# Strassen's output projection in layer B: raw weights and attention outputs loaded ahead of their splits

## The chip, the cores and the metric

The kernel runs on one core of a Trainium2 chip. The metric is the device time of one execution in microseconds. An A/B difference under about 0.2% (4 us here) can't be told from none.

## The reference

One inference step of two encoder layers over 2048 prompt tokens and 64 sample tokens, width 1024. Each layer is

```python
h = rms_norm(x, norm_g)
q, k, v, gate = split(h @ w_in)            # q and k normalised per head
o = attend(q, k, v, bias, band of chunks)  # 16 heads of 64
x = x + (o * silu(gate)) @ w_out           # w_out: 1024 x 1024
```

Layer A attends over its own and 2 earlier chunks of 64 tokens, layer B over its own and 8 earlier. The case concerns the last line for layer B, the output projection `y = x1 + og @ w_out_b` over 2112 tokens, everything in float32 outside the kernel.

## The kernel before, in words

**Precision by splitting.** TensorE multiplies float16. Each float32 operand is split into a high and a low float16 part, and a product is three matmuls: high by high, high by low, low by high. A split is one instruction on ScalarE (`hi = scale * raw`, L2130 for weights, L2192 for attention outputs) and then one on VectorE (`lo = scale * raw - hi`, L2131 and L2195).

**The projection** (`fast_output_jobs`). The tokens are cut into 8 spans of 264 (`OT`). The first two spans are done one by one (`alone`; here "the first block" and "the second block"): for each of 8 output chunks of 128, two products of 12 matmuls of 264 columns, one for each half of the inner dimension. The other six spans are done in three pairs (`group`) by a Strassen scheme with seven products of 12 matmuls for each of 4 output chunks, instead of eight. A *combine* (L2284, VectorE) adds a finished product from PSUM, with a scale, to the residual tile `res` or `more`; after its last combine a tile is stored. Two accumulator banks alternate, so a product can begin only when the combine two before it is done. The first and second block have 8 combines each, every pair 28.

**Operands.** 16 weight tiles of 128 x 512 are split as they are (`plain`), and 16 more are sums and differences of raw weight tiles (`mixed`: four for each output chunk `m`, made on GpSimd, L2153). A pair's outputs need seven tiles of two halves each: four raw quarters per half come into the four `xraw` buffers (`fetch_half`), three subtractions on GpSimd (L2243) change them in place between the splits, and a fourth follows for the last tile. A second half is loaded into the same four buffers.

**What sets the order.** The PE queue is written in program order. All other engines' queues, SP's included (it issues every DMA), are ordered at build time by a scheduler that simulates the program, within its dependences and extra ordering edges (`behind`). Layer B's attention (`pipeline`) interleaves scores, exponentials and P times V with the projections (`filler`). Into each of its steps `drip` puts one or two *steps* of the two chains `drips["x"]` (output splits) and `drips["w"]` (weight splits), x first; a product forces those of its own operands that have not run (`force`). The chain of weights is opened by `held["prepare"]`, called from `scale_work` in the last head pair (hp 7) at its eighth event, once the weight scale is known. Each split step loads its own raw tile (`raw_w`) and splits it:

```python
def plain(m, b):
    def fn():
        st.w[m, b].w = split_w(raw_w(m, b))     # wraw: 3 buffers
    st.w[m, b] = Step("w", fn)
```

Names in the trace: `wraw`, `xraw` raw tiles; `wx`, `ws` (4 buffers each), `wh`, `wl` (12 each) split weights; `xx` (7 buffers), `ph`, `pl`, `values`, `pt` split outputs, the last four tags borrowed from attention; `pj` accumulators; `p` attention scores (3 buffers); `sb` score banks.

Of the kernel before, what the change touches and what calls it, by code (L numbers as in the profile page):

```python
# [14 lines left out]
ALU = mybir.AluOpType  # L15
AX = mybir.AxisListType

P = 128
# [16 lines left out]
WB = 3  # L35
# [4 lines left out]
WN = 12  # L40
# [18 lines left out]
def hybrid_encoder_kernel(  # L59
# [246 lines left out]
    def scale_work(hp, u, e):  # L306
# [20 lines left out]
        elif at == 2:  # L327
            output_top()
        elif at == 3:
            held["chain"].append(output_across)  # L330
        elif at == 5:
            held["chain"].append(output_scales)
        elif at == 8:
            while held["chain"]:
                held["chain"].pop(0)()
            held["prepare"]()
# [1757 lines left out]

    def drip(n=1):
        for _ in range(n):
            for chain in drips.values():
                if chain:
                    chain[0].run()
                    break  # L2100
# [16 lines left out]
    def fast_output_jobs(xin, xout):  # L2117
# [4 lines left out]
        wtags = ["wx"] * 4 + ["wh"] * 4 + ["wl"] * 4 + ["ws"] * 4 + ["wh"] * 8 + ["wl"] * 8  # L2122
        both = 2 * OT
        step = 3 * OT / 2400
        spans = [(0, 1), (1, 1)] + [(2 + 2 * p, 2) for p in range(3)]

# [7 lines left out]
        def raw_w(m, b):  # L2134
            raw = t("wraw", [P, 512], WB)
            load(raw.rearrange("p (k c) -> p k c", k=4), w_o_b[m, :, b])
            return raw

        def plain(m, b):
            def fn():  # L2140
                st.w[m, b].w = split_w(raw_w(m, b))
            st.w[m, b] = Step("w", fn)

        def mixed(m):
            raws = {}

            def put(i, fn):
                def run():
                    st.s[m, i].w = split_w(fn())
                st.s[m, i] = Step("w", run)  # L2150

            def pool(dst, x, y_, op):
                nc.gpsimd.tensor_tensor(raws[dst], raws[x], raws[y_], op=op)  # L2153
                return raws[dst]

            def s1():
                for b in (2, 3, 0):
                    raws[b] = raw_w(m, b)
                return pool(3, 2, 3, ALU.add)

            def s4():
                raws[1] = raw_w(m, 1)
                return pool(1, 1, 0, ALU.subtract)

            put(4, s1)
            put(6, lambda: pool(2, 0, 2, ALU.subtract))
            put(5, lambda: pool(0, 3, 0, ALU.subtract))
            put(2, s4)

        def prepare():  # L2170
            run_all("scales")
            for b in range(0, 4, 2):
                for m in range(4):
                    for e in range(2):
                        plain(m, b + e)
            for m in range(4):
                mixed(m)
# [3 lines left out]
        def fetch(j, n, c):  # L2181
            out = []
            for s in range(n):
# [3 lines left out]
                out.append(raw)  # L2187
            return out
# [20 lines left out]
        def operand(i):  # L2209
# [18 lines left out]
            tags = ["values"] * 3 + ["pt"] * 2 + ["xx"] * 2 if i == 3 else ["xx"] * 5 + ["ph", "pl"]  # L2228
# [6 lines left out]
            def split(y_, k, at, less=()):  # L2235
                def part(e):
                    if k == 0 and e:
                        fetch_half(e)
# [3 lines left out]
                    for o, a, b in less:  # L2242
                        nc.gpsimd.tensor_tensor(raws[e, o], raws[e, a], raws[e, b], op=ALU.subtract)  # L2243
                    split_x(x.parts[y_][:, 2 * e : 2 * e + 2], raws[e, at], tag in ("ph", "pl") and e == 0)
                return part
# [73 lines left out]
        def group(i, x, m):  # L2319
# [6 lines left out]
            for y_, (acc, wi, xi, start, rv) in enumerate((  # L2326
# [7 lines left out]
                if not filler.attending and (y_ % 2 or m == 3):  # L2334
                    drip()
                if wi == 2:
                    store(xout[:, m, rows], top)
                    next_res(i, m)
# [7 lines left out]
        def add_span(i):  # L2346
# [7 lines left out]
            def gen():  # L2354
# [6 lines left out]
                for m in range(4) if n == 2 else range(0, 8, 2):  # L2361
                    if ready(i + 1) and (i or m == 4):
                        st.x[i + 1] = operand(i + 1)
                    yield from (group if n == 2 else alone)(i, x, m)
# [129 lines left out]
```

## Time and profile before

| | us |
|---|---|
| median of 3 runs | 2090.42 (2086.74 to 2090.99) |
| profiled execution | 2088.68 |
| its span, first to last instruction | 2086.9 |
| mean granted TensorE clock | 0.992 |
| first product of the projection starts | 1879.87 |
| last matmul ends about | 2083.3 |
| a matmul of 264 columns, start to start | 0.113 |

In a timeline row stand the start, the duration, the engine, the line, the operation and the tiles written and read; in square brackets the idle time of that engine before it and what ended it. `PE` is TensorE, `DVE` VectorE, `ACT` ScalarE, `POOL` GpSimd, `SPq` the queue that issues DMAs. A row of waits reads: who waited, for whom, total us, times, longest.

### The profile page before, as it was taken

To read this page: it belongs to the slowest core of one execution; us is meant where nothing else is said; L and a number is where in the kernel's file an instruction comes from. 1 tells how busy PE (TensorE), PEld (TensorE's weight loads), DVE (VectorE), ACT (ScalarE), POOL (GpSimd) and SP (SyncE) were. 2 spreads that over 40 slices of the span, in tenths; PEclk is the share of its full clock that TensorE was granted. 3 is DMA by queue.
4 is the path that set the end of the run, shared out by engine and by line. 5 is a ranking of instruction groups with operands and counts; after the bars stand their busy time and mean duration, and the time that the engine had idled before them with its cause. 6 is when DMAs were issued, how large, how long until landed. Compare 5 with 4: busy or idle time off the path is not lost.

```text
span 2086.9 us, 40567 instructions
## 1 busy us (share of the span) xinstructions
PE 1987.4 (95%) x12670; PEld 1416.2 (68%) x12670; DVE 1448.5 (69%) x4111; ACT 1440.5 (69%) x3574; POOL 1191.9 (57%) x1569
## 2 busy tenths in 40 slices
PE   7899999999999999989999999999999999989699
PEld 6787787777888999645555555555555555557578
DVE  7667767767667554778667676776767767687763
ACT  6887888778788332468777787777867778786420
POOL 5665565444457445677566565765756666566620
PEclk9999999999999999999999999999999999999899
DMA  7888877889766776798989798897978878598543
GB/s 258 254 216 229 222 202 207 225 208 271 194 170 169 220 224 196 266 239 219 240 173 242 169 218 200 187 237 168 226 186 199 215 163 184 139 198 189 169 146 105
DMA packets 598168, 424.64 MB, mean 203 GB/s; under 512 B 403952, under 2 KB 527232, under 8 KB 597920
## 3 DMA queue, kind: packets, MB, share of 16 engines
q1 hardware_dynamic: 597952, 422.06, 78.9%
q8 instruction: 100, 1.64, 0.3%
q14 instruction: 116, 0.95, 0.2%
HBM read 253.14 MB, written 73.43 MB: 156 GB/s over the span
## 4 chain that ended last, share of the span: by engine, by line
PE 50%; DVE 10%; DMA 8%; ACT 6%; issue 5%; POOL 2%; SPq 1%; ACTq 0%; POOLq 0%; DVEq 0%
PE pj L758 9%; PE pj L760 9%; PE pj L759 9%; PE o L1847 4%; PE sb L1683 2%; PE sb L1684 2%; PE pj L2059 2%; PE pj L2061 2%; PE pj L2060 2%; PE tp L1011 1%; PE pj L2291 1%; PE pj L2294 1%; PE pj L2295 1%; DVE p L1687 1%; DMA q<-q 1%
## 5 line engine op out<-in xcount | busy, mean ns | idle before, releaser
L758 PE MATMUL pj<-wh,xx 128*128 128x512 f16 (+2 forms) x1648 | 642.2, 390 | 19.7 <-ACT pa L781 4.4
L760 PE MATMUL pj<-wh,xx 128*128 128x512 f16 (+2 forms) x1648 | 624.5, 379 | 0.6 <-POOL xx L640 0.6
L1740 POOL TENSOR_TENSOR values<-p,values 128x640 f16<-128x640 f32 (+4 forms) x256 | 327.0, 1278 | 199.1 <-ACT values L1739 190.6
L759 PE MATMUL pj<-wh,xx 128*128 128x512 f16 x1024 | 388.9, 380 | 1.3 <-DVE wh L545 1.3
L1699 ACT ACTIVATE p<-p,nm 128x640 f32<-128x640 f32 (+5 forms) x264 | 199.5, 756 | 182.4 <-DVE nm L1692 146.6
L1687 DVE CUSTOM_DVE_ANT_0 p<-sb,BT 128x640 f32<-128x640 f32 (+5 forms) x272 | 196.4, 722 | 141.9 <-PE sb L1684 120.5
L640 POOL TENSOR_TENSOR xx<-xraw,xx 128x528 fp32r<-128x528 f32 (+4 forms) x144 | 188.5, 1329 | 94.7 <-ACT xx L639 87.5
L759 PE MATMUL pj<-wl,xx 128*128 128x512 f32 (+1 forms) x624 | 235.3, 377 | 1.5 <-DVE wl L545 1.5
L849 POOL TENSOR_TENSOR f<-f,mhalf 128x4 f32<-128x4 f32 x182 | 186.3, 1024 | 12.2
L760 PEld LDWEIGHTS <-xx 128*128 128x128 f16 x1024 | 100.4, 98 | 124.1 <-issue 2.7
L1347 ACT ACTIVATE p<-p,nm 128x257 f32<-128x257 f32 (+2 forms) x272 | 134.5, 496 | 68.7 <-DVE nm L1336 35.7
L1500 POOL TENSOR_TENSOR o<-gt,o 128x256 f32<-128x256 f32 (+1 forms) x132 | 106.1, 804 | 125.0 <-ACT p L1347 72.7
L1739 ACT CAST values<-p 128x640 f16<-128x640 f32 (+4 forms) x256 | 168.2, 657 | 12.9 <-DMA pt<-values 6.8
L758 PEld LDWEIGHTS <-xx 128*128 128x128 f16 x1024 | 100.3, 98 | 83.8 <-ACT sq L827 1.4
L759 PEld LDWEIGHTS <-xx 128*128 128x128 f16 x1024 | 100.4, 98 | 83.3 <-issue 3.5
L2059 PE MATMUL pj<-xx,wh 128*128 128x264 f32 x512 | 148.5, 290 | 4.3 <-DVE res L2069 1.8
L1847 PEld LDWEIGHTS <-values 128*128 128x128 f16 x1344 | 123.8, 98 | 39.6 <-DMA pt<-values 1.7
L1847 PE MATMUL o<-pt,values 128*128 128x256 f16 (+1 forms) x1344 | 144.7, 256 | 2.2 <-DMA pt<-values 2.2
L2060 PE MATMUL pj<-xx,wh 128*128 128x264 f32 x512 | 145.7, 285 | 0.0
L2061 PE MATMUL pj<-xx,wl 128*128 128x264 f32 x512 | 145.0, 283 | 0.2 <-DVE wl L538 0.2
L758 PEld LDWEIGHTS pj<-wh,xx 128*128 128x128 f32 x624 | 119.2, 191 | 36.9 <-ACT pa L781 8.2
L760 PEld LDWEIGHTS pj<-wh,xx 128*128 128x128 f32 x624 | 119.0, 191 | 23.1
(356 smaller groups left out, 5082.5 us busy)
## 6 DMA issues: line engine op xcount, KB each, us to landing
xx<-xsb SPq DMA_DIRECT2D x112, 512.0 KB, 4.3
xx<-xsa SPq DMA_DIRECT2D x88, 512.0 KB, 4.9
xraw<-oga SPq DMA_DIRECT2D x64, 264.0 KB, 3.8
xsa<-xx SPq DMA_DIRECT2D x32, 512.0 KB, 4.0
wl<-in_w_in_b_dram SPq DMA_DIRECT2D x64, 256.0 KB, 5.1
wraw<-in_w_in_b_dram SPq DMA_DIRECT2D x56, 256.0 KB, 3.6
wraw<-in_w_o_b_dram SPq DMA_DIRECT2D x48, 256.0 KB, 4.0
xraw<-in_x_dram SPq DMA_DIRECT2D x40, 256.0 KB, 4.3
```

The costliest lines, as they stand in the source:

```text
L640: nc.gpsimd.tensor_tensor(lo, rv, wide(hi), op=ALU.subtract)
L758: nc.tensor.matmul(ps[:n, :C], xh, wh, start=k == 0, stop=False)
L759: nc.tensor.matmul(ps[:n, :C], xh, wl, start=False, stop=False)
L760: nc.tensor.matmul(ps[:n, :C], xl, wh, start=False, stop=k == KC - 1)
L849: nc.gpsimd.tensor_tensor(fv, fv, mhalf[:n, :H], op=ALU.pow)
L1687: mi = nc.vector.tensor_tensor_reduce(out=p[r, :nk], in0=S[r, o : o + nk], in1=b, op0=ALU.add, op1=ALU.min, scale=1.0, scalar=3e38, accum_ ...
L1699: ex = nc.scalar.activation(p[:n, :nk], p[:n, :nk], AF.Exp, scale=-1.0, bias=it.nm[:n, c : c + 1], accum_out=it.sm[:n, c : c + 1],)
L1740: lo = nc.gpsimd.tensor_tensor(two[:, :, 1, :], pv, two[:, :, 0, :], op=ALU.subtract)
L1847: nc.tensor.matmul(it.O[:, h * T + q0 : h * T + q1_], held["VH"][:, kt, h], x, start=kt == kb and not low, stop=kt == tb and low == 1,)
L2059: nc.tensor.matmul(ps[:, :OT], wh, oh, start=k == 0, stop=False)
L2060: nc.tensor.matmul(ps[:, :OT], wh, ol, start=False, stop=False)
L2061: nc.tensor.matmul(ps[:, :OT], wl, oh, start=False, stop=k == KC - 1)
```

## The change

- `prepare` runs at the sixth event of the last head pair instead of the eighth, and loads three raw weight tiles itself; every single split then loads the tile three splits ahead (`ahead`).
- The raw tiles of the mixed weights come four at a time, several steps ahead (`late`: after splits 10, 16, 20 and 26), into buffers of their own: `wl` for m 0 and 1, `wraw` and `scan` for 2, `p` and `wraw` for 3.
- `gate_at` keeps a chain from dripping for some ticks after its loads; while x waits, w drips. `pin` adds an ordering edge to the loads and subtractions: not ahead of the latest anchor.
- The tiles' tags come in another order (`ws` second; `ph`, `pl` fourth and fifth).
- In the first block, before its last group (m 6), the second block's remaining splits are forced and the first pair's operand (`operand(2)`) is begun. The second half's raws are asked for at the end of the first half.
- Outside attention a pair drips one step at every product (was: at products 1, 3, 5, and at all in the last group). The next group's residuals are loaded after the third product instead of the sixth.

No arithmetic changes, and the PE queue keeps its order of matmuls in the projection.

```diff
-        elif at == 8:
+        elif at == 6:
             while held["chain"]:
                 held["chain"].pop(0)()
             held["prepare"]()
...
+    gate_at, ticks = {"x": 0, "w": 0}, [0]
+
     def drip(n=1):
+        ticks[0] += 1
         for _ in range(n):
-            for chain in drips.values():
-                if chain:
+            for kind, chain in drips.items():
+                if chain and ticks[0] >= gate_at[kind]:
                     chain[0].run()
                     break
...
-        wtags = ["wx"] * 4 + ["wh"] * 4 + ["wl"] * 4 + ["ws"] * 4 + ["wh"] * 8 + ["wl"] * 8
+        wtags = ["wx"] * 4 + ["ws"] * 4 + ["wh"] * 4 + ["wl"] * 4 + ["wh"] * 8 + ["wl"] * 8
...
+        def pin(x):
+            behind(x.ins, list(bg.anchors.values())[-1])
...
+        def raw_w(key, tag, bufs):
+            cols = 640 if tag == "p" else 512
+            raw = t(tag, [P, cols], bufs)[:, :512]
+            pin(load(raw.rearrange("p (k c) -> p k c", k=4), w_o_b[key[1], :, key[2]]))
+            raws_w[key] = raw
+
+        singles = [(0, m, b + e) for b in range(0, 4, 2) for m in range(4) for e in range(2)]
+
+        def mixed_raws(m):
+            tags = [("wl", WN)] * 4 if m < 2 else [("wraw", WB)] * 3 + [("scan", 1)]
+            if m == 3:
+                tags = [("p", 3)] * 3 + [("wraw", WB)]
+            for b, tag in zip((2, 3, 0, 1), tags):
+                raw_w((1, m, b), *tag)
+
+        ahead = {n: (lambda n=n: raw_w(singles[n + 3], "wraw", WB)) for n in range(13)}
+        late = {10: 0, 16: 1, 20: 2, 26: 3}
+
+        def order_w(store_in, key, fn):
+            n = len(drips["w"])
+
+            def run():
+                store_in[key].w = split_w(fn())
+                if n in ahead:
+                    ahead[n]()
+                if n in late:
+                    mixed_raws(late[n])
+
+            store_in[key] = Step("w", run)
 
         def prepare():
             run_all("scales")
+            for n in range(3):
+                raw_w(singles[n], "wraw", WB)
+            gate_at["w"] = ticks[0] + 2
...
                 held["last"] = load(raw, og[1][:, c : c + 2, o : o + OT]).ins
                 out.append(raw)
+            gate_at["x"] = ticks[0] + (1 if filler.attending else 3)
             return out
...
-            tags = ["values"] * 3 + ["pt"] * 2 + ["xx"] * 2 if i == 3 else ["xx"] * 5 + ["ph", "pl"]
+            tags = ["values"] * 3 + ["pt"] * 2 + ["xx"] * 2 if i == 3 else ["xx"] * 3 + ["ph", "pl"] + ["xx"] * 2
...
-                    if k == 0 and e:
-                        fetch_half(e)
...
+                    if y_ == 5 and e == 0:
+                        fetch_half(1)
...
-                if not filler.attending and (y_ % 2 or m == 3):
+                if not filler.attending:
                     drip()
+                if wi == 5:
+                    next_res(i, m)
                 if wi == 2:
                     store(xout[:, m, rows], top)
-                    next_res(i, m)
...
+                    if i == 0 and m == 6:
+                        for chain in st.x[1].steps.values():
+                            force(*chain)
+                        st.x[2] = operand(2)
```

How the queues come out is shown at two places. The lines of the changed kernel are some higher: L2136 and L2137 are its weight splits, L2204 and L2207 its output splits, L2145 and L2197 the loads of weight and output raws, L2182 and L2253 the subtractions, L2296 the combine, L2279 the residual loads of the single blocks.

The first place is the end of the first block. `res_25682` (after: `res_25712`) takes the eighth combine, the first block's last, and `more_25799` (`more_25837`) the ninth; `p`, `nm` and `o` rows are attention. VectorE before:

```order
L2131 SCALAR_TENSOR_TENSOR wh_25839<-wraw_25548,scl,wh_25839 128x512
L1692 TENSOR_SCALAR nm_25747<-nm_25747 128x1
L2284 SCALAR_TENSOR_TENSOR res_25682<-pj_25844,scl,res_25682 128x264
L2131 SCALAR_TENSOR_TENSOR wh_25880<-wraw_25877,scl,wh_25880 128x512
L1687 ISA p_25930,nm_25747<-sb_25929,BT 128x640
L1687 ISA nm_25747 128x1
L1499 TENSOR_TENSOR o_4936_25900<-o_25786,o_4936_25900 64x256 x2
L1692 TENSOR_SCALAR nm_25747<-nm_25747 128x1
L1811 TENSOR_TENSOR o_4948_25966<-tp_25959,o_4948_25966 64x64 x2
L2284 SCALAR_TENSOR_TENSOR more_25799<-pj_25919,scl,more_25799 128x264
```

VectorE after:

```order
L2207 SCALAR_TENSOR_TENSOR xx_25876<-xraw_25829,scl,xx_25876 128x2x264
L1692 TENSOR_SCALAR nm_25777<-nm_25777 128x1
L2207 SCALAR_TENSOR_TENSOR xx_25879<-xraw_25833,scl,xx_25879 128x2x264
L2296 SCALAR_TENSOR_TENSOR res_25712<-pj_25884,scl,res_25712 128x264
L2207 SCALAR_TENSOR_TENSOR xx_25917<-xraw_25835,scl,xx_25917 128x2x264
L1687 ISA p_25965,nm_25777<-sb_25964,BT 128x640
L1687 ISA nm_25777 128x1
L1499 TENSOR_TENSOR o_4953_25943<-o_25816,o_4953_25943 64x256 x2
L1692 TENSOR_SCALAR nm_25777<-nm_25777 128x1
L1811 TENSOR_TENSOR o_4961_26001<-tp_25994,o_4961_26001 64x64 x2
L2296 SCALAR_TENSOR_TENSOR more_25837<-pj_25954,scl,more_25837 128x264
```

Three splits of the first pair's outputs stand where two splits of mixed weights stood; those weights are split earlier. GpSimd at the same place, from the cast of the last but one score tile on, before:

```order
L1740 TENSOR_TENSOR values_11787<-p_25855,values_11787 128x5x128
L2153 TENSOR_TENSOR wraw_26270<-wraw_26268,wraw_26270 128x512
L1500 TENSOR_TENSOR o_4936_25900<-gt_25898,o_4936_25900 128x256
L2153 TENSOR_TENSOR wraw_26268<-wraw_26272,wraw_26268 128x512
L1812 TENSOR_TENSOR o_4948_25966<-G_25652,o_4948_25966 128x64
L1724 TENSOR_TENSOR G_26018<-pb_25192,sm_25746 128x128 x2
L1740 TENSOR_TENSOR values_11787<-p_25930,values_11787 128x5x128
L2153 TENSOR_TENSOR wraw_26272<-wraw_26270,wraw_26272 128x512
L2243 TENSOR_TENSOR xraw_25909<-xraw_25911,xraw_25909 128x528
```

GpSimd after:

```order
L2253 TENSOR_TENSOR xraw_25829<-xraw_25831,xraw_25829 128x528
L1740 TENSOR_TENSOR values_11787<-p_25895,values_11787 128x5x128
L2253 TENSOR_TENSOR xraw_25831<-xraw_25835,xraw_25831 128x528
L2253 TENSOR_TENSOR xraw_25835<-xraw_25835,xraw_25829 128x528
L1500 TENSOR_TENSOR o_4953_25943<-gt_25941,o_4953_25943 128x256
L1812 TENSOR_TENSOR o_4961_26001<-G_25682,o_4961_26001 128x64
L2182 TENSOR_TENSOR wl_25382<-wl_25386,wl_25382 128x512
L2182 TENSOR_TENSOR wraw_25623<-wraw_25621,wraw_25623 128x512
L1724 TENSOR_TENSOR G_26053<-pb_25217,sm_25776 128x128 x2
L2253 TENSOR_TENSOR xraw_25833<-xraw_25833,xraw_25835 128x528
L1740 TENSOR_TENSOR values_11787<-p_25965,values_11787 128x5x128
```

The first pair's subtractions stand up to eight rows further forward, one ahead of the cast. ScalarE there, after (before, no split stood between the two exponentials but that of `wh_25839`):

```order
L2204 ACTIVATE xx_25876<-xraw_25829,scl 128x2x264
L2204 ACTIVATE xx_25879<-xraw_25833,scl 128x2x264
L1699 ACTIVATE p_25895,sm_25776<-p_25895,nm_25777 128x640
L1495 COPY o_4953_25943<-o_25816 64x256 x2
L1739 CAST values_11787<-p_25895 128x5x128
L2204 ACTIVATE xx_25917<-xraw_25835,scl 128x2x264
```

Two output splits moved ahead of the last exponential but one. SP's queue where the first pair's raws are issued, before:

```order
L2316 DMA out_dram<-res_25436 128x2x264
L2186 DMA xraw_25909<-ogb 128x2x264
L1507 DMA ogb<-o_4895_25616 128x256
L2186 DMA xraw_25911<-ogb 128x2x264
L2267 DMA res_25917<-x_99 128x2x264
L2316 DMA out_dram<-more_25560 128x2x264
L2267 DMA more_26008<-x_99 128x2x264
L2186 DMA xraw_25913<-ogb 128x2x264
L2186 DMA xraw_25915<-ogb 128x2x264
```

SP after:

```order
L2328 DMA out_dram<-res_25465 128x2x264
L1748 DMA_TRANSPOSE pt_25649<-values_11787 128x10x128
L2197 DMA xraw_25829<-ogb 128x2x264
L2197 DMA xraw_25831<-ogb 128x2x264
L2279 DMA res_25952<-x_99 128x2x264
L2328 DMA out_dram<-more_25582 128x2x264
L2279 DMA more_26043<-x_99 128x2x264
L2197 DMA xraw_25833<-ogb 128x2x264
L2197 DMA xraw_25835<-ogb 128x2x264
```

The four raws keep their place among the stores and reloads. The second place is in the second block, VectorE from its third combine (`res`, the eleventh of all) on. Before:

```order
L2284 SCALAR_TENSOR_TENSOR res_25917<-pj_26010,scl,res_25917 128x264
L2131 SCALAR_TENSOR_TENSOR wh_26430<-wraw_26272,scl,wh_26430 128x512
L2195 SCALAR_TENSOR_TENSOR ph_26060<-xraw_25911,scl,ph_26060 128x2x264
L2284 SCALAR_TENSOR_TENSOR res_25917<-pj_26050,scl,res_25917 128x264
L2195 SCALAR_TENSOR_TENSOR xx_26024<-xraw_25915,scl,xx_26024 128x2x264
```

After:

```order
L2296 SCALAR_TENSOR_TENSOR res_25952<-pj_26045,scl,res_25952 128x264
L2207 SCALAR_TENSOR_TENSOR xx_25876<-xraw_26060,scl,xx_25876 128x2x264
L2207 SCALAR_TENSOR_TENSOR xx_26056<-xraw_25833,scl,xx_26056 128x2x264
L2207 SCALAR_TENSOR_TENSOR xx_25879<-xraw_26064,scl,xx_25879 128x2x264
L2296 SCALAR_TENSOR_TENSOR res_25952<-pj_26092,scl,res_25952 128x264
```

The second half's splits have come forward to between these two combines; `xraw_26064` takes over a buffer of the first half.

More of the change, by code (lines that the diff above doesn't have):

```diff
@@ L2132, in split_w @@
             return w
[L2134 to L2168, printed above, removed]
+        raws_w = {}
@@ L2170, in prepare @@
+        ahead = {n: (lambda n=n: raw_w(singles[n + 3], "wraw", WB)) for n in range(13)}
[9 more added lines that the diff above has]
+            store_in[key] = Step("w", run)
         def prepare():
             run_all("scales")
[L2172 to L2175, printed above, removed]
@@ L2176, in prepare, with pool @@
-            for m in range(4):
-                mixed(m)
+            for n in range(3):
+                raw_w(singles[n], "wraw", WB)
+            gate_at["w"] = ticks[0] + 2
+            for key in singles:
+                order_w(st.w, key[1:], lambda key=key: raws_w[key])
+            for m in range(4):
+                def pool(dst, x, y_, op, m=m):
+                    r = [raws_w.get((1, m, b)) for b in (dst, x, y_)]
+                    pin(nc.gpsimd.tensor_tensor(*r, op=op))
+                    return r[0]
+                order_w(st.s, (m, 4), lambda pool=pool: pool(3, 2, 3, ALU.add))
+                order_w(st.s, (m, 6), lambda pool=pool: pool(2, 0, 2, ALU.subtract))
+                order_w(st.s, (m, 5), lambda pool=pool: pool(0, 3, 0, ALU.subtract))
+                order_w(st.s, (m, 2), lambda pool=pool: pool(1, 1, 0, ALU.subtract))
@@ L2242, in part @@
                     for o, a, b in less:
-                        nc.gpsimd.tensor_tensor(raws[e, o], raws[e, a], raws[e, b], op=ALU.subtract)
+                        pin(nc.gpsimd.tensor_tensor(raws[e, o], raws[e, a], raws[e, b], op=ALU.subtract))
                     split_x(x.parts[y_][:, 2 * e : 2 * e + 2], raws[e, at], tag in ("ph", "pl") and e == 0)
+                    if y_ == 5 and e == 0:
+                        fetch_half(1)
                 return part
```

## The prediction

> **What bounds the kernel now.** I read the page first: the busy table, then the 40 slices.
>
> ```profile
> PE 1987.4 (95%) x12670; PEld 1416.2 (68%) x12670; DVE 1448.5 (69%) x4111; ACT 1440.5 (69%) x3574; POOL 1191.9 (57%) x1569
> PE   7899999999999999989999999999999999989699
> PEclk9999999999999999999999999999999999999899
> ```
>
> TensorE is busy 95% of the span; apart from the first slice its weakest slice is the third from the end, where layer B's output projection takes over from attention. Everything the change touches lies between 1800 us and the end, so the second view is the same span in stretches (engine busy us, matmul count in brackets, granted clock, DMA share).
>
> ```profile
> 1810.00:1820.00 10.00, 10.00 (x61) 5.71 (x59) 6.82 (x20) 7.76 (x18) 6.13 (x9) 1.00 0.43 91
> 1860.00:1870.00 10.00, 9.96 (x59) 5.46 (x58) 8.68 (x22) 8.51 (x18) 9.67 (x12) 1.00 1.05 187
> 1870.00:1880.00 10.00, 7.93 (x42) 4.20 (x40) 9.33 (x24) 9.78 (x22) 5.51 (x7) 0.85 1.02 248
> 1913.00:1920.00 7.00, 7.00 (x64) 6.07 (x62) 4.56 (x11) 4.95 (x13) 1.71 (x2) 1.00 1.04 221
> 1920.00:1985.00 65.00, 47.08 (x350) 36.58 (x348) 50.64 (x62) 28.49 (x44) 45.49 (x34) 0.89 0.60 162
> 1985.00:1994.00 9.00, 9.00 (x82) 7.83 (x81) 4.72 (x9) 0.73 (x1) 0.52 (x1) 1.00 0.77 240
> 1994.00:2018.00 24.00, 20.04 (x170) 16.33 (x169) 20.08 (x28) 10.07 (x14) 11.48 (x8) 1.00 0.44 136
> 2018.00:2087.00 69.00, 65.27 (x581) 56.53 (x578) 24.43 (x50) 0.00 (x0) 0.00 (x0) 1.00 0.33 107
> ```
>
> (Columns: PE, PEld, DVE, ACT, POOL, clock, DMA, GB/s.) The stretch 1920 to 1985, second block and first pair, loses 65 - 47.08 = 17.9 us of TensorE time, and its clock of 0.89 another 0.11 x 65 = 7.2 us at most. 1994 to 2018 loses 4.0. The rest is full. Who is waited for in the 65 us:
>
> ```profile
> PE pj L2291 <- DVE res L2284: 12.6, 8, 3.4
> POOL wraw L2153 <- DMA wraw<-in_w_o_b_dram: 11.5, 6, 3.8
> ACT values L2192 <- DMA xraw<-ogb: 9.5, 4, 2.9
> DVE wl L2131 <- ACT wl L2130: 4.9, 2, 2.8
> DVE wh L2131 <- ACT wh L2130: 3.5, 2, 3.2
> ```
>
> TensorE waits for combines (L2284: accumulator into the residual). A combine is short; it is late because splits stand ahead of it in VectorE's queue. The groups of that window by line (count | busy us, mean ns | idle before them and its releaser), and then the same few microseconds in GpSimd's and in VectorE's timeline (start, duration):
>
> ```profile
> L2195 DVE SCALAR_TENSOR_TENSOR xx<-xraw,scl,xx 128x528 f16<-128x528 f32 x13 | 15.5, 1217 | 1.3 <-ACT xx L2192 1.2
> L2131 DVE SCALAR_TENSOR_TENSOR wl<-wraw,scl,wl 128x512 f16<-128x512 f32 x8 | 9.1, 1141 | 4.9 <-ACT wl L2130 4.9
> L2195 DVE SCALAR_TENSOR_TENSOR values<-xraw,scl,values 128x528 f16<-128x528 f32 x6 | 5.6, 934 | 3.3 <-ACT values L2192 3.3
> L2131 DVE SCALAR_TENSOR_TENSOR wh<-wraw,scl,wh 128x512 f16<-128x512 f32 x4 | 4.1, 1050 | 3.5 <-ACT wh L2130 3.5
> L2284 DVE SCALAR_TENSOR_TENSOR res<-pj,scl,res 128x264 f32<-128x264 f32 x13 | 6.2, 479 | 0.0
> ...
> L2243 POOL TENSOR_TENSOR xraw<-xraw,xraw 128x528 f32<-128x528 f32 x16 | 23.8, 1485 | 8.4 <-DVE wl L2131 4.1 <-DVE values L2195 2.7 <-DMA xraw<-ogb 1.3
> L2153 POOL TENSOR_TENSOR wraw<-wraw,wraw 128x512 f32<-128x512 f32 x12 | 17.1, 1427 | 14.8 <-DMA wraw<-in_w_o_b_dram 11.5 <-DVE o L1499 3.3
> ```
>
> ```profile
> 1944.57 1.73 POOL L2153 TENSOR_TENSOR wraw<-wraw,wraw 128x512 f32<-128x512 f32 x1
> 1946.26 1.79 POOL L2243 TENSOR_TENSOR xraw<-xraw,xraw 128x528 f32<-128x528 f32 x1
> 1948.02 1.73 POOL L2153 TENSOR_TENSOR wraw<-wraw,wraw 128x512 f32<-128x512 f32 x1
> 1954.94 1.26 POOL L2153 TENSOR_TENSOR wraw<-wraw,wraw 128x512 f32<-128x512 f32 x1 [3.48 <-DMA wraw<-in_w_o_b_dram]
> ```
>
> ```profile
> 1944.34 4.28 DVE L2195 SCALAR_TENSOR_TENSOR xx<-xraw,scl,xx 128x528 f16<-128x528 f32 x3
> 1948.54 1.75 DVE L2131 SCALAR_TENSOR_TENSOR wl<-wraw,scl,wl 128x512 f16<-128x512 f32 x1
> 1976.39 0.73 DVE L2131 SCALAR_TENSOR_TENSOR wl<-wraw,scl,wl 128x512 f16<-128x512 f32 x1
> ```
>
> The weight split takes 0.73 us at 1976, while GpSimd is idle, and 1.75 at 1948, beside a GpSimd subtraction; that subtraction takes 1.26 alone (1954.94) and 1.73 beside the split. The pair side by side costs 1.75 where one after the other would cost 1.99: the two engines nearly take turns. So the stretch is bound by the splits and subtractions together, 42.8 us of splits (the four groups above and 8.5 us in three smaller ones, 38 splits) and 40.9 us of 28 subtractions in 65 us, and to a lesser part by raw tiles that come late.
>
> **The change, part by part.**
>
> Start earlier (event 6 for 8, raws 3 splits ahead). The first weight split moves about four score steps forward, to near 1810, where VectorE has 3.2 us of 10 idle, ScalarE 2.2 and DMA stands at 0.43: cost 0, covered by that slack. Without it each split would cost up to 1.75. Counted in the queues up to the ninth combine (1918.57 in the trace, the first of the second block), before has done 20 weight splits and no split of the first pair, after 21 and 3: four fewer remain. GpSimd has two subtractions fewer behind the same attention cast, and the next two are of outputs, which need no weight raw; they fit in the 3.76 us in which it now stands idle:
>
> ```profile
> 1919.70 1.27 POOL L2153 TENSOR_TENSOR wraw<-wraw,wraw 128x512 f32<-128x512 f32 x1 [3.76 <-DMA wraw<-in_w_o_b_dram]
> ```
>
> ```profile
> 1918.57 0.49 DVE L2284 SCALAR_TENSOR_TENSOR more<-pj,scl,more 128x264 f32<-128x264 f32 x1
> ```
>
> So four subtractions fewer too. Four splits at the mean 42.8/38 = 1.13 us are 4.5, four subtractions at 40.9/28 = 1.46 are 5.8. If they overlap wholly the stretch shrinks by 5.8, if not at all by 10.3; since they nearly take turns I take 8.0.
>
> Mixed raws in buffers of their own (wl, p, scan): the 11.5 us of GpSimd's waits for weight raws go. What of that reached VectorE is its own idle time for wh and wl, 4.9 + 3.5 = 8.4. Bounds 0 and 8.4. Late next are the output raws, still four buffers filled in halves, so I take half: 4.2.
>
> First pair's operands in the first block. The order shows what this does not move: the third and fourth raw (xraw_25833, 25835) still stand on SP behind the reload of "more", which waits for its own store.
>
> ```profile
> 1906.30 0.42 SPq L2316 DMA_DIRECT2D out_dram<-more  x1
> 1909.76 0.36 SPq L2267 DMA_DIRECT2D more<-x  x1
> 1910.21 0.94 SPq L2186 DMA_DIRECT2D xraw<-ogb  x2
> ```
>
> Beside SP's timeline, the table of transfers (us to landing, last column) and ScalarE's timeline:
>
> ```profile
> xraw<-ogb SPq DMA_DIRECT2D x28, 264.0 KB, 4.1
> ```
>
> ```profile
> 1912.46 0.83 ACT L1699 ACTIVATE p<-p,nm 128x640 f32<-128x640 f32 x1 [1.50 <-DVE nm L1692]
> ```
>
> They land at about 1910.2 + 4.1 = 1914.3. The split of xraw_25833 now stands ahead of an attention exponential on ScalarE and of the eighth combine on VectorE. Behind the first wait the cast, GpSimd's part of it, the transposes and the last P times V products; it slips from 1912.46 to about 1915, 2.5 us. TensorE has single products of the second block to run meanwhile, so I charge 0 (bound 2.5). In the second half xraw_26064 is loaded only when GpSimd has finished with xraw_25833, and its split stands directly ahead of the twelfth combine: 0.4 issue + 4.1 landing + 0.7 ScalarE = 5.2 us, of which about 2.2 are covered by the split ahead of it. New wait: +3.0 (bounds 0 and 5.2).
>
> Drips at every product, residual loads three products earlier, tags in another order: the built order of the last pair's splits is the same within a row or two, and the loads were not waited for by TensorE. 0 in 1994 to 2018, bounds -4.0 (its idle) and +3 (one SP reload with its store wait ahead of three raws).
>
> Sum: -8.0 - 4.2 + 3.0 = -9.2 us. The profiled execution took 2088.68 (its span is 2086.9); the median of the three runs stands 1.74 above it. 2088.68 - 9.2 = 2079.5, as a median 2081.
>
> The row on taking turns has a rule behind it: the Trainium skill, "SBUF — State Buffer", section on the two separate sides, says VectorE (with two SBUF inputs) and a reading GpSimd share one port pair as an exclusive lock, held for the whole instruction. The trace agrees for splits (0.73 against 1.75) and for combines, which read one input from PSUM and keep 0.48. By it alone loads could not shorten the stretch, and only moved work would count: -8.0, so 2082.
>
> **The rivals.**
>
> (A) The late raws are the bound. For it: 11.5 us of waits, the longest 3.8, and the clock, which falls behind the long gaps. Against: VectorE is idle for only 14.4 of the 65 us. If all of that goes besides the work, 14.4 + 8.0 = 22 us: 2068.
>
> (B) It doesn't do what it says. For it: the pair's raws stand where they stood on SP, and the new waits (3.0, and 2.5 of attention) come in. With their upper bounds, -8.0 + 5.2 + 2.5: 2090.
>
> (C) Slower: DMA. Up to the fourth combine's store SP now issues 28 weight raws, before 21; two groups of four go out at once, near 1845 and 1885, into DMA shares of 0.99 to 1.05 from 1860 to 1890. 256 KB at 187 to 248 GB/s is 1.1 to 1.4 us, so a group can hold the transposes and query copies up by 5.6 us, and as at 1876 a gap of 2 us is followed by a slow clock:
>
> ```profile
> 1876.58 0.32 PE L1683 MATMUL sb<-KA,q 128*128 128x384 f16 x1 [2.07 <-ACT ws L2130]
> 1877.31 0.63 PE L758 MATMUL pj<-wh,xx 128*128 128x512 f16 x1
> ```
>
> (0.63 us where 0.38 is usual.) Two such stalls, each with some 3.4 us of half clock behind it (1876.58 to 1880, six long matmuls and a score), so 1.7 us lost, are 2 x 7.3 = 14.6 us: 2081 + 14.6 = 2096. It outweighs the gain once the new idle time in 1840 to 1900 passes 9.2 us, and measurably so at 13.4. Against it: at a DMA share of 1.05 (1860 to 1870) TensorE was busy 9.96 of 10 us.
>
> **How the numbers follow.** Forecast 0.52, A 0.21, B 0.17, C 0.10. The forecast's own range is -16 to -4.3, 2074 to 2086; with A and most of B the range is 2066 to 2091, which leaves out the rest of A and most of C, about 0.15. What a measurement can tell from no change is 0.2%, 4.2 us. Faster: forecast and A, 0.73. Same: B, 0.17. Slower: C, 0.10.
>
> **What would show it.** Right: in the stretch from the ninth to the thirty-first combine, TensorE idle near 9 us rather than 17.9, hardly a GpSimd wait on weight raws, the split of a raw such as xraw_26064 with a DMA wait ahead of the twelfth combine, GpSimd subtractions still 1.7 us beside splits; 1800 to 1900 as before. Wrong: idle under 3 us there with full clock (A), new "DMA xraw" waits as long as the old (B), or TensorE waiting for pt or q before 1900 (C).

## Result and the profile after

The changed kernel takes 2082.43 us (median of 22 runs), the kernel before 2086.45 in the same comparison (22 runs): a ratio of 0.9978, 95% interval 0.9967 to 0.9988. The medians lie 4.0 us apart; the ratio says 4.6 us faster (2.5 to 6.9). A second comparison gave 0.9968 (0.9956 to 0.9979), 6.7 us. The forecast was 2081, but from a median of 2090.42 over three runs; as a difference it was -9.2, and between 0.4 and 0.7 of that came. In the experiments one run of a_dve_mix (7181 us) and one of a_p_raws (10402 us) are left out of the ratios as slow.

The page of the changed kernel, busy table and slices:

```profile
PE 1984.7 (95%) x12670; PEld 1416.7 (68%) x12670; DVE 1450.5 (70%) x4111; ACT 1440.2 (69%) x3574; POOL 1198.2 (57%) x1569
PE   7898999999999999989999999999999999999699
PEclk9999999999999999999999999999999999999999
```

The same instructions are compared below, not the same microseconds: the stretches begin and end at the transposes of L210 in the last head pair (14 us before the first weight load of the changed kernel), at the ninth, the thirty-first and the fifty-third combine, and at the end. Before:

```profile
1784.55:1918.57 134.02, 127.34 (x864) 82.90 (x865) 102.91 (x264) 101.67 (x237) 79.73 (x95) 0.99 0.82 175
1918.57:1984.68 66.11, 48.32 (x361) 37.65 (x359) 50.99 (x63) 29.89 (x47) 45.48 (x34) 0.90 0.61 166
1984.68:2019.86 35.18, 31.09 (x266) 25.95 (x266) 25.94 (x39) 10.80 (x15) 12.32 (x9) 1.00 0.52 163
```

After:

```profile
1789.45:1924.44 134.99, 128.22 (x871) 83.45 (x872) 104.53 (x268) 103.73 (x241) 86.62 (x99) 0.99 0.86 195
1924.44:1983.44 59.00, 41.80 (x355) 34.16 (x354) 52.45 (x61) 28.23 (x44) 44.85 (x31) 1.00 0.52 147
1983.44:2017.61 34.17, 31.27 (x269) 26.08 (x268) 24.73 (x38) 10.29 (x14) 11.48 (x8) 1.00 0.54 175
```

The second row holds the gain: 66.1 becomes 59.0. TensorE's idle time in it is almost what it was (17.8 before, 17.2 now), while its clock went from 0.90 to 1.00 and its busy time fell by 6.5; VectorE's idle time fell from 15.1 to 6.6, while its busy time did not fall. Also, the first trace of the changed kernel is 4.9 us late already at L210, before anything that the change touches, so the spans (2086.9 and 2084.3) hide most of it.

The waits in that stretch of the changed kernel:

```profile
PE pj L2303 <- DVE res L2296: 12.4, 10, 3.0
POOL xraw L2253 <- DMA xraw<-ogb: 11.1, 3, 5.4
ACT values L2204 <- DMA xraw<-ogb: 10.6, 6, 3.3
ACT xx L2204 <- POOL xraw L2253: 7.0, 6, 2.7
ACT xx L2204 <- DMA xraw<-ogb: 6.2, 3, 2.4
```

GpSimd waits for no weight raw any more (11.5 us before); raw outputs are waited for, by GpSimd and by ScalarE. GpSimd's and VectorE's timelines in its middle:

```profile
1940.74 1.73 POOL L2182 TENSOR_TENSOR wl<-wl,wl 128x512 f32<-128x512 f32 x1
1942.43 1.71 POOL L2182 TENSOR_TENSOR wraw<-wraw,wraw 128x512 f32<-128x512 f32 x1
1944.10 1.73 POOL L2182 TENSOR_TENSOR p<-p,p 128x512 f32<-128x512 f32 x1
1945.79 1.75 POOL L2253 TENSOR_TENSOR xraw<-xraw,xraw 128x528 f32<-128x528 f32 x1
1947.51 1.71 POOL L2182 TENSOR_TENSOR scan<-scan,wraw 128x512 f32<-128x512 f32 x1
```

```profile
1941.66 1.35 DVE L2137 SCALAR_TENSOR_TENSOR wl<-wraw,scl,wl 128x512 f16<-128x512 f32 x1
1942.94 1.77 DVE L2207 SCALAR_TENSOR_TENSOR pl<-xraw,scl,pl 128x528 f16<-128x528 f32 x1
1944.63 0.84 DVE L1499 TENSOR_TENSOR o<-o,o 64x256 f32<-64x256 f32 x2
1945.50 0.88 DVE L2137 SCALAR_TENSOR_TENSOR wh<-wl,scl,wh 128x512 f16<-128x512 f32 x1
1946.30 0.48 DVE L2296 SCALAR_TENSOR_TENSOR more<-pj,scl,more 128x264 f32<-128x264 f32 x1
```

In this part of the stretch GpSimd stands in one unbroken row of subtractions, each at its long duration, and most splits beside them are long too. Over the whole stretch it is still idle for 14.2 of 59.0 us (20.6 of 66.1 before).

### The profile page after: what moved, and what is told of

Read it like the earlier page. It is cut to its first block, busy times and chain, and to the rows that moved or that the text cites. A ratio compares the mean times of both kernels' runs of the same rounds, so it can differ in the third digit from the quotient of the medians.

```text
span 2084.3 us, 40524 instructions
## 1 busy us (share of the span) xinstructions
PE 1984.7 (95%) x12670; PEld 1416.7 (68%) x12670; DVE 1450.5 (70%) x4111; ACT 1440.2 (69%) x3574; POOL 1198.2 (57%) x1569
## 4 chain that ended last, share of the span: by engine, by line
PE 49%; DVE 11%; ACT 6%; DMA 6%; issue 5%; POOL 3%; SPq 1%; ACTq 0%; DVEq 0%; POOLq 0%
PE pj L758 9%; PE pj L760 9%; PE pj L759 9%; PE o L1847 4%; PE pj L2059 2%; PE sb L1683 2%; PE pj L2061 2%; PE pj L2060 2%; PE sb L1684 2%; PE tp L1011 1%; PE pj L2303 1%; DVE p L1687 1%; PE pj L2307 1%; PE pj L2306 1%; DMA xraw<-ogb 1%
## 5 line engine op out<-in xcount | busy, mean ns | idle before, releaser
L1347 ACT ACTIVATE p<-p,nm 128x257 f32<-128x257 f32 (+2 forms) x272 | 134.4, 496 | 68.0 <-DVE nm L1336 34.7
```

## The experiments

Readings were tested against each other. M, the prediction's main term: each split and subtraction moved ahead of the stretch shortens it. R: the raw weights are late, and VectorE's idle time behind them is what went. Once the first runs were in, there were two more for what is left: P, splits on VectorE and subtractions on GpSimd take turns; D, raw tiles still land late.

For each trace, in us (from the starts of the combines in VectorE's timeline; c7 is the seventh combine; `splits` is how many splits VectorE begins between c9 and c31, `split` the mean of one; a ratio is to the kernel before, and the last four rest on 2 to 6 runs each):

| kernel | L210 at | L210 to c7 | c7 to c9 | c9 to c31 | c31 to c53 | splits | split | ratio of times |
|---|---|---|---|---|---|---|---|---|
| before | 1784.55 | 123.9 | 10.1 | 66.1 | 35.2 | 38 | 1.13 | |
| before_again | 1784.42 | 123.8 | 10.1 | 63.0 | 34.7 | 38 | 1.20 | |
| after | 1789.45 | 124.0 | 11.0 | 59.0 | 34.2 | 35 | 1.26 | 0.9978 |
| after_again | 1784.98 | 127.3 | 10.7 | 58.7 | 34.0 | 35 | 1.25 | 0.9968 |
| b_event6 | 1778.55 | 127.2 | 10.1 | 58.9 | 34.6 | 35 | 1.17 | 0.9989 |
| a_weights | 1783.01 | 124.7 | 9.0 | 60.2 | 34.0 | 36 | 1.13 | 0.9976 |
| b_outputs | 1780.28 | 124.2 | 11.2 | 58.1 | 38.4 | 38 | 1.18 | 0.9990 |
| a_no_pair | 1778.42 | 124.3 | 9.0 | 60.4 | 33.7 | 36 | 1.20 | 0.9966 |
| a_p_raws | 1782.17 | 124.8 | 11.5 | 57.1 | 34.1 | 36 | 1.23 | 0.9979 |
| a_dve_mix | 1783.75 | 123.7 | 11.7 | 60.5 | 34.0 | 36 | 1.05 | 0.9985 |
| a_short_pe | 1789.01 | 124.0 | 9.7 | 50.7 | 32.6 | 30 | 1.29 | 0.9924 |
| a_memset | 1784.46 | 124.5 | 10.5 | 55.2 | 34.0 | 35 | 0.80 | 0.9949 |
| a_small_sub | 1784.70 | 123.5 | 11.3 | 46.6 | 31.2 | 35 | 0.79 | 0.9903 |
| b_small_sub | 1790.11 | 123.0 | 10.1 | 56.2 | 32.0 | 40 | 0.79 | 0.9957 |

**after_again: the changed kernel unchanged.** 

> The changed kernel once more, to see which part of its first trace belongs to the kernel. Both theories: 2 to 6 us below before in total. If the 59.0 us from the ninth to the thirty-first combine (before: 66.1) are a property of the kernel, they come again within 1.5 us; if they were luck of that execution, 62 or more. If the 4.9 us that the first trace lies behind before at the transposes of L210 (1789.45 against 1784.55, ahead of every instruction the change touches) are chance, that row stands somewhere from 1780 to 1790 here, without relation to the change.

59.0 came again as 58.7, so it belongs to the kernel. L210 stands at 1784.98: the 4.9 us were chance, and over all traces that row lies anywhere from 1778.4 to 1790.1. The ratio, 0.9968, is 6.7 us, just above the 2 to 6 expected.

**before_again: the kernel before unchanged.** 

> The kernel before once more, for a second trace. If the 66.1 us from its ninth to its thirty-first combine (clock 0.90) belong to the kernel, 64.5 to 67.5 again, and the three part changes really took 6 to 8 us out of this stretch. If they were a slow execution of it (it took 2 to 4 us more than the median of its runs), 61 to 64, and the gain of every part is smaller than the first traces say.

```profile
1918.31:1981.30 62.99, 48.13 (x361) 37.73 (x359) 53.53 (x64) 30.16 (x47) 45.10 (x34) 0.89 0.58 168
```

63.0 is the second answer: the first trace caught one of the longer executions of before. Before stands at 63 to 66, so the stretch gains 4 to 7 us (means 64.55 and 58.86: 5.7), not 7.1. With two traces of each kernel, a difference of 3 us between single traces proves little.

**The parts alone.** `b_event6` is the kernel before with one line changed:

```diff
-        elif at == 8:
+        elif at == 6:
```

> The kernel before with nothing but the earlier start (sixth event for eighth). In its built order 24 weight splits stand ahead of the ninth combine, against 20 before. Theory M (moved work, the -8.0 of the prediction: four splits and their subtractions less in the stretch): 58 to 62 us from the ninth to the thirty-first combine, total -4 to -8. Theory R (the raws are late for GpSimd, and VectorE's idle time behind that is what went): every split still loads its own raw, so 65 to 67 us and a total within 2 us of before.

`a_weights` is the changed kernel with the output half undone (abridged; the tags and `next_res` go back as well):

```diff
-            gate_at["x"] = ticks[0] + (1 if filler.attending else 3)
...
+                    if k == 0 and e:
+                        fetch_half(e)
...
-                    if y_ == 5 and e == 0:
-                        fetch_half(1)
...
-                if not filler.attending:
+                if not filler.attending and (y_ % 2 or m == 3):
                     drip()
...
-                    if i == 0 and m == 6:
-                        for chain in st.x[1].steps.values():
-                            force(*chain)
-                        st.x[2] = operand(2)
```

> The changed kernel with its weight half alone: the sixth event, raws of single weights three splits ahead, raws of mixed weights in buffers of their own; the output operands, their tags, the drips and the residual loads as before. 23 weight splits stand ahead of the ninth combine (before 20, changed 21 and three output splits). Theory M: as the earlier start alone gives, 58 to 62 us. Theory R: this is the part that counts, GpSimd's waits for weight raws go from 11.5 us to under 2, 59 to 61 us and total -4 to -7, while the earlier start alone gives nothing.

`b_outputs` is the kernel before with just those output lines of the change put in. 

> The kernel before with the output half alone: the first pair's operand begun in the first block, second half's raws asked for at the end of the first half, the tags' order, a drip at every product, residual loads later, x's gate; weights as before. 18 weight and 11 output splits stand ahead of the ninth combine (before 20 and 8). Theory M: one split more ahead, -1 to -2 us. Theory R: the weight raws stay late and the weights now come later still, 66 to 70 us, total 0 to +4.

```profile
1915.86:1974.72 58.86, 43.92 (x363) 35.35 (x361) 49.41 (x61) 28.05 (x44) 40.31 (x29) 0.97 0.58 159
1916.75:1976.99 60.24, 47.28 (x382) 38.42 (x380) 49.47 (x62) 28.13 (x45) 42.89 (x31) 0.94 0.57 157
1915.68:1973.83 58.15, 43.67 (x353) 34.94 (x353) 52.53 (x63) 29.20 (x46) 43.61 (x30) 0.97 0.73 198
```

(In this order, one fence line from each kernel's table of stretches.) Neither theory holds for all three. M has the stretch right for the earlier start (58.9) and the weight half (60.2), R only for the weight half; neither allowed for the output half (58.1). The weight half, of which the earlier start is one line, and the output half share no part, yet each part alone brings the stretch to 58 to 60, and all together no further. They also get there in different ways. The earlier start has three splits fewer in it (35) and VectorE idle for 9.5 us, with nothing loaded ahead; the output half has as many splits as before (38) and VectorE idle for only 5.6. From c7 to c31 the three stand at 69.0, 69.2 and 69.3, the whole change at 70.0 and 69.4, before at 76.2 and 73.1. Their totals differ, though the intervals overlap or touch, and two losses elsewhere are seen in the traces. The earlier start alone (0.9989, interval 0.9976 to 1.0002; a total of -4 to -8 was expected) has a longer stall in attention, at the place that the prediction named for its rival C (2.07 us before, clock slow at both):

```profile
1865.28 4.16 DVE L2195 SCALAR_TENSOR_TENSOR xx<-xraw,scl,xx 128x528 f16<-128x528 f32 x1
1872.90 0.48 PE L1683 MATMUL sb<-KA,q 128*128 128x384 f16 x1 [4.63 <-DVE nm L1687]
```

This does not look like rival C's mechanism: VectorE, which TensorE waits for, was held up there not by a DMA but by a split that took 4.16 us, while GpSimd ran five instructions without a gap.

The output half alone (0.9990, 0.9980 to 1.0000) leaves the last mixed weight late, behind c31, and takes 3 to 4 us more than before from c31 to c53:

```profile
1977.68 0.75 DVE L2134 SCALAR_TENSOR_TENSOR wl<-wraw,scl,wl 128x512 f16<-128x512 f32 x1 [3.36 <-ACT wl L2133]
```

The weight half alone gives 0.9976 (0.9964 to 0.9988), as much as all of it within the intervals.

**a_no_pair: without the pair's operand in the first block.**

```diff
-                    if i == 0 and m == 6:
-                        for chain in st.x[1].steps.values():
-                            force(*chain)
-                        st.x[2] = operand(2)
```

> The changed kernel without the four lines that force the second block's splits and begin the first pair's operand in the first block. 23 weight and 8 output splits stand ahead of the ninth combine (changed: 21 and 11), 67 in all ahead of the thirty-first, as in the changed kernel. Theory P (the stretch has a floor of splits and subtractions taking turns, which each part alone reaches): 58 to 61 us, the total as the changed kernel within 2 us. Theory M (each moved split counts, -8.0 in all): one split fewer ahead of the stretch, 60 to 62, total 1 to 2 us above the changed kernel.

60.4 fits both theories; the total of 0.9966 (0.9953 to 0.9979) is P's and shows no gain from this part. It shortens c9 to c31 by 1.4 to 1.7 and lengthens c7 to c9 from 9.0 to 11.0 and 10.7. The reason is in ScalarE's timeline of the changed kernel:

```profile
1917.19 0.73 ACT L2204 ACTIVATE xx<-xraw,scl 128x528 f16<-128x528 f32 x1 [1.22 <-DMA xraw<-ogb]
1917.83 0.81 ACT L1699 ACTIVATE p<-p,nm 128x640 f32<-128x640 f32 x1
```

The split of the third raw waits for its load, and an exponential of attention behind it.

**a_short_pe: is it TensorE?**

```diff
-                nc.tensor.matmul(acc, wh, lo, start=False, stop=False, skip_group_check=True)
...
+                if not short:
+                    nc.tensor.matmul(acc, wh, lo, start=False, stop=False, skip_group_check=True)
...
```

(Abridged: the third matmul stands under `if not short` as well, and `short` holds in the second block and the first pair.)

> The changed kernel with the second block's and first pair's products cut to 4 of their 12 matmuls (high by high alone). The combines then come earlier in the built order: 61 of the splits stand ahead of the thirty-first, against 67. Read to the same split, the 67th: theory P and D both say that TensorE is only waiting here, so from the ninth combine to that split it takes what it took (59 us) within 3 us. Theory C (the slow clock and TensorE's own work hold the stretch): it falls by 10 us or more.

The combines come earlier (c31 after 30 splits), so the same split has to be compared: from the ninth combine to the end of the 35th split behind it 59.9 us, against 58.7 and 58.4. With a third of the matmuls nothing got shorter up to that split: TensorE's work does not hold the changed kernel's stretch. What the half clock of before (0.90 and 0.89) cost was not tested by itself.

**a_small_sub and b_small_sub: short subtractions.**

```diff
-                        pin(nc.gpsimd.tensor_tensor(raws[e, o], raws[e, a], raws[e, b], op=ALU.subtract))
+                        pin(nc.gpsimd.tensor_tensor(*[raws[e, z][:, :, :8] for z in (o, a, b)], op=ALU.subtract))
```

and the same with `[:, :16]` for the weights (in the kernel before without `pin`). 

> The changed kernel with every subtraction on GpSimd cut to 16 columns of 512 or 528 (it leaves out the rest of each difference); loads, splits and their order stay, except that splits come a few places earlier where the scheduler sees the subtraction as short. All parts alone and together end at 58.2 to 60.2 us from the ninth to the thirty-first combine. Theory P (what is left is splits and subtractions taking turns): splits fall to 0.74 us everywhere, VectorE's work in the stretch to 35 x 0.74 + 23 x 0.48 + 2 = 39 us, and the stretch to TensorE's 42 us of work and some waits, 44 to 50. Theory D (what is left are raw tiles that land late): the same loads wait for the same stores and buffers, 55 to 59.

> The kernel before with the same cut subtractions. Theory P: 66.1 falls as far as in the changed kernel, less the idle time that late raws leave: 50 to 54. Theory D (in the kernel before the late raws alone made the difference): 62 to 66.

```profile
1919.55:1966.11 46.56, 40.44 (x353) 34.18 (x353) 36.06 (x61) 25.13 (x41) 12.37 (x30) 1.00 0.71 210
1923.21:1979.40 56.19, 43.44 (x362) 35.45 (x361) 40.21 (x65) 29.48 (x48) 16.06 (x34) 0.97 0.72 209
POOL wraw L2153 <- DMA wraw<-in_w_o_b_dram: 17.3, 7, 4.2
```

(The third line is from the waits of b_small_sub.) Splits fall to 0.79 us, and the stretch to 46.6 in the changed kernel, as theory P said. In the kernel before it falls only to 56.2, which is neither P's 50 to 54 nor D's 62 to 66; there GpSimd still waits 17.3 us for weight raws. With GpSimd light the two kernels lie 9.6 us apart in the stretch, with the subtractions as they are 5.7. How much of the 3.9 between is taken back by longer splits is not shown, since b_small_sub also has 40 splits in the stretch, and a_small_sub 35.

**a_dve_mix: weight subtractions on VectorE.**

```diff
-    pin(nc.gpsimd.tensor_tensor(*r, op=op))
+    pin(nc.vector.tensor_tensor(*r, op=op))
```

> The changed kernel with the 16 subtractions of weights on VectorE instead of GpSimd. About 9 of them stand between the ninth and the thirty-first combine. If the two engines take turns (theory P), 0.74 of VectorE takes the place of 1.73 of GpSimd and the splits beside them fall to 0.74 us: 56 to 60 us, although VectorE has more to do, and splits of 0.9 to 1.1 us on average (changed: 1.27 and 1.30). If VectorE's own work were the limit and GpSimd's runs beside it (theory V), the 9 subtractions come on top: 59 + 9 x 0.74 = 65 to 66.

```profile
1919.16:1979.66 60.50, 46.20 (x353) 36.58 (x353) 53.94 (x73) 27.52 (x44) 26.91 (x20) 0.92 0.55 163
L2182 DVE TENSOR_TENSOR wraw<-wraw,wraw 128x512 f32<-128x512 f32 x3 | 3.3, 1088 | 0.0
```

VectorE took over eleven subtractions, 9.2 us in all (the costliest group is the second line), and was busy 53.9 us, 1.5 to 1.9 more than in the changed kernel: the splits paid for most of it, falling from 1.26 to 1.05. 60.5 is far from theory V's 65 and just above P's range; 5.5 of VectorE's 6.6 us of idle time now stand behind TensorE. No gain either way (0.9985, 0.9967 to 1.0003).

**a_p_raws: raw outputs earlier.** The second pair's second half goes into `p` buffers:

```diff
-                    if y_ == 5 and e == 0:
+                    if y_ == 5 and e == 0 and i != 3:
                         fetch_half(1)
+                    if y_ == 0 and e == 0 and i == 3:
+                        fetch_more((0, 0), (1, 0), (1, 1))
+                    if y_ == 3 and e == 0 and i == 3:
+                        fetch_more((0, 1))
```

(Abridged: `fetch_more` loads the first three into `p` buffers and the last into an `xraw` buffer.)

> The changed kernel with three of the four raw outputs of the second pair's second half in the score buffers p, free by then, asked for after the operand's first split instead of after its last but one (the fourth still follows in an xraw buffer). After 1959 us the changed kernel's GpSimd waits 11 us for raw outputs and VectorE idles 4 to 5 us behind ScalarE. Theory D (late raws hold the rest): from the sixteenth to the thirty-first combine 25 to 27 us instead of 29, from there to the fifty-third 33 instead of 34, total 3 to 5 us below the changed kernel. Theory P: the raws come earlier, the subtractions with them, and the splits beside them get longer: under 2 us.

57.1, of it 27.3 from c16 to c31 (29.2 and 29.0 in the changed kernel), where D said 25 to 27: the stretch is 1.8 us shorter, inside the "under 2" of theory P, and this is not seen in the total (0.9979, 0.9964 to 0.9993).

**a_memset: GpSimd occupied, but not reading.**

```diff
-    pin(nc.gpsimd.tensor_tensor(*r, op=op))
+    pin(nc.gpsimd.tensor_tensor(*[x[:, :16] for x in r], op=op))
+    for _ in range(2):
+        pin(nc.gpsimd.memset(r[0], 0.0))
```

(The weights' subtractions; those of the outputs change in the same way.)

> The changed kernel with every subtraction on GpSimd replaced by one of 16 columns and two memsets of the whole tile, which write and read nothing (it leaves out the differences; the tiles hold zeros). GpSimd stays occupied, some 0.36 + 2 x 0.53 = 1.4 us for each (rows of the small subtraction and of a memset of 128x512), ScalarE waits for it as before, and the built order of splits is that of the changed kernel within one row. Theory P (VectorE's splits are held up by what GpSimd reads and writes at the same time): if reading is what counts, splits fall to about 0.8 us and the ninth to the thirty-first combine take 46 to 51 us; if writing counts as well, splits of 1.1 to 1.3 and 56 to 59. Theory L (it is the hand-off, the time that GpSimd keeps ScalarE and VectorE waiting for a difference): splits of 0.8, and nevertheless 54 to 59.

```profile
1919.42:1974.61 55.19, 44.65 (x359) 36.40 (x358) 36.31 (x60) 26.98 (x44) 34.94 (x79) 0.94 0.61 172
L2209 DVE SCALAR_TENSOR_TENSOR xx<-xraw,scl,xx 128x528 f16<-128x528 f32 x10 | 7.6, 764 | 6.3 <-ACT xx L2206 6.3
L2207 DVE SCALAR_TENSOR_TENSOR xx<-xraw,scl,xx 128x528 f16<-128x528 f32 x10 | 14.1, 1421 | 0.5 <-ACT xx L2204 0.5
ACT values L2206 <- DMA xraw<-ogb: 13.1, 4, 5.4
ACT xx L2206 <- DMA xraw<-ogb: 9.0, 3, 4.0
```

(The third line is the same group in the changed kernel.) The numbers that came are theory L's, not P's. The splits take 0.80 us on average, the ten `xx` splits 0.76 against 1.42, although GpSimd is busy 34.9 us beside them: neither GpSimd's being busy nor its writing stretches them, but the reading subtractions do. Yet the stretch still takes 55.2, only 3.7 us less. The 16 us that VectorE saves turn into 18.9 us of idle time (6.6 in the changed kernel), most of it behind ScalarE, which now waits 22.1 us for raw outputs (16.8 in the changed kernel). So taking turns is not the only limit. A second one lies a few microseconds below it, and its likely place is the four output buffers, each filled, subtracted, split and filled again. No run tests that by itself, and a_p_raws, which gave three raws other buffers, gained 1.8 us. Only where GpSimd neither reads for long nor is occupied for long does the stretch come down to 46.6. How much of these last 8.6 us is the shorter subtraction and how much the few splits that the scheduler then puts earlier stays open.

## Why the prediction was right, and where its sum was not

The direction and the place held: the gain lies between the ninth and the thirty-first combine, and attention and the last pair gave nothing beyond 1 us that the repeated traces confirm. The size is at the weak end of the forecast's own range of -4.3 to -16: the first comparison has 4.0 us by its medians, just short of the range, and 4.6 by its ratio, the second 6.7. That 2082.43 lies so near to 2081 is luck: the kernel before, run more often, stands 4 us lower than the median that the sum started from, and the gain is smaller by about as much. By terms, on two traces of each kernel:

- **Moved work, -8.0: 0 in the whole change,** if it is read from VectorE's busy time (51.0 and 53.5 us before, 52.5 and 52.0 after). Three splits and three subtractions fewer stand in the stretch (38 became 35, 28 became 25), not four and four, and above all the price was wrong. Splits summed to 42.9 and 45.5 us before and to 44.2 and 43.8 after. The term took before's mean of 1.13 as the price of a split. But that price depends on how much GpSimd does beside it: GpSimd was idle for 31% and 28% of the stretch before and for 24% after, and each remaining split takes 1.26 and 1.25. The prediction had the rows (0.73 alone, 1.75 beside) and did not ask what the second term would do to the first.
- **Raw waits, -4.2: -5.7,** if all of VectorE's idle time is counted: 15.1 and 9.5 us before, 6.6 and 6.7 after. Its idle time behind `wh` and `wl`, from which the term came, was 8.4 in one trace of before, 2.4 in the other, and none after.
- **Which of these two made the gain stays open.** Counted per split, the stretch took 1.74 and 1.66 us before, 1.69 and 1.68 after, and 1.68 in b_event6, where nothing is loaded ahead; three splits fewer at that rate are 5.0 us, nearly all of 5.7. But b_outputs is as short with 38 splits, at 1.53 each. Either way alone is enough, and the sum of the two terms, -12.2, was not to be had.
- **New wait at the twelfth combine, +3.0: 0.** ScalarE does wait 2.4 us there for raws, but VectorE is never idle at that place; the three splits ahead of c12 run back to back, 4.88 us. The prediction counted 2.2 us of cover from one of them, and the three covered the whole wait.
- **Attention behind the third raw, charged 0 (bound 2.5): about +2** against the kernel without this part (c7 to c9), and 0.6 to 0.9 against before. So "first pair's operands in the first block" is a part that pays for itself and no more.
- **1994 to 2018, 0: about -0.9** (c31 to c53 34.95, then 34.1).

Of the signs to look for, "TensorE idle near 9 us" was wrong: it is 17.2 and 16.5 still (17.8 and 14.9 before), since the clock became full and TensorE's busy time fell along with the stretch. "Hardly a wait on weight raws", "a raw such as xraw_26064 awaited" and "subtractions 1.7 us beside splits" came. "1800 to 1900 as before" held in one trace; in the other the part from L210 to c7 is 3.4 us longer. Rival A fell at its price of 22 us: in a_weights no weight raw is late and the stretch is still 60. Late output raws remain (22.1 us of ScalarE's waits in a_memset), but bringing three of them earlier gained only 1.8. Rival B fell with the total. C's mechanism is seen in small: in after_again a cast waits 1.87 us for a transpose and, further on, TensorE stands for 3.36, and in a_weights and a_p_raws TensorE waits 2.35 and 2.33 us for q; none of this comes near its deciding 9.2.

The row on turns and the rule beside it: the Trainium skill, "SBUF — State Buffer", section on the two separate sides, gives a lock held for the whole instruction between VectorE with two SBUF inputs and a GpSimd instruction that reads. The runs agree that reading is the condition (splits of 0.80 us beside memsets, 1.26 beside subtractions) and that an input from PSUM is free of it (combines 0.48 to 0.49 throughout). That 2082.43 was measured is no support for the 2082 that the prediction drew from moved work alone: that sum too stood on 2090.42, and b_outputs gained in the stretch without having fewer splits in it.

## What to carry to other kernels

When two engines take turns on a resource, a price read from a trace in which one of them starves is too low: feeding the starved one raises the other's price (here from 1.13 and 1.20 us to 1.26 and 1.25), so work moved and waits removed must not be added. Several parts that each reach the same limit are not worth their sum; run each alone, and keep the one that loses nothing measurable elsewhere (here the weight half). And measure a change in the last tenth of a kernel from an anchor just ahead of it: here the part before the anchor scattered by 12 us, three times the effect.

## What the hardware showed unasked

A slow clock does not follow from a gap's length alone. In the changed kernel 2.15 us of idle time before 1881.71 are followed by a granted clock of 0.50 from 1881.92 to 1885.33, and these two longer gaps by none (0.27 us is the usual duration here, about 0.42 the slow one):

```profile
1954.76 0.27 PE L2303 MATMUL pj<-xx,wx 128*128 128x264 f16 x1 [3.01 <-DVE res L2296]
1958.84 0.27 PE L2303 MATMUL pj<-ph,wh 128*128 128x264 f16 x1 [2.57 <-DVE res L2296]
```

In a_p_raws the first of them, again of 3.01 us, was followed by half clock:

```profile
1948.80 0.27 PE L2315 MATMUL pj<-xx,wx 128*128 128x264 f16 x1 [3.01 <-DVE res L2308]
1949.90:1956.73 6.83, 4.53 (x22) 3.00 (x21) 6.83 (x10) 3.22 (x5) 3.08 (x2) 0.50 0.72 232
```

What decides is where the gap lies. Within each trace the half-clock intervals behind L210 begin on one grid of 3.41 us, and each lasts 3.41 us or a whole multiple, unless the program ends first; in each of the 14 traces the grid lies elsewhere. Cut by that grid, the stretches of 3.41 us at full clock in which TensorE idled 2.06 us or more were followed by half clock in 35 of 35 cases, those with 1.95 us or less in none of 1069; five lay between and went both ways. The grid divided the 3.01 us into 1.85 and 1.16 in the changed kernel, while 2.31 of them fell into one stretch in a_p_raws. The Trainium skill, "TensorE: Matmul & The Clock Gate", Part 1 on the clock gate, says that activity is judged in windows of 3.4 us that run free of the program; the clock records agree. So whether a gap of 2 to 4 us costs half clock changes from run to run.
